# When the retention outputs of a two-layer hybrid step are issued: two lanes started earlier, gating statistics read from a copy, pooling split over two turns

## The chip, the cores and the metric

The kernel runs on one core of one Trainium2 chip. The metric is the device time of one launch in microseconds (us). The time before is 1567.13 us, the median of three runs (1566.71 to 1568.31).

Engines are named as in the profile: PE is TensorE, PEld its weight loads, DVE VectorE, ACT ScalarE, POOL GpSimd, SP the queue that issues most DMAs. Each engine carries out its own instructions strictly in the order in which they were written; between engines there are only semaphores.

## The reference

Two layers of a hybrid network work on 640 tokens of width 1024: one chunk of 128 context tokens and four chunks of 128 latent tokens, called chunk 0 to chunk 4. Everything is float32. Each layer projects its input once, and the columns feed four mixers:

- A: windowed attention.
- B: spatial gating. Of v, 256 wide, every token is normalised (mean and variance over the 256 values), a 128 x 128 matrix mixes the tokens of a chunk, and the result is multiplied with u.
- C: retention. For each chunk, head and direction the output is `(q k^T * decay) v + (q * q_dec) state`. It is normalised per head and multiplied with silu of a gate, and the two directions are added.
- D: pooling. Centred means over windows of 2, 4, 8 and 16 tokens minus the token itself, then a small matrix per group. Near a sequence's two ends the mean has fewer tokens, so eight columns at each edge are multiplied with a correction.

The four results go through one output projection, a residual and a layer norm, and then through a gated convolutional feed-forward block.

## The kernel before, in words

Every large product is done in three float32r passes (high part times high part, low times high, high times low). `fm_mm` (L576) makes a feature-major block of 128 output features, `tm_mm` (L840) a token-major block of one chunk by 256 features. 640 columns don't fit one PSUM bank, so each feature-major unit comes as a wide block (384 columns) and a narrow block (256 columns), 24 matmuls each. A `Stream` (L239 to L290) splits the weights ahead of use: one ACT copy `wh` and one DVE subtraction `wl` are issued whenever a unit is freed. It also puts in the matmuls of later modulations (`ada`).

The order of the work is written out by hand. Nothing is reordered after that. Between the blocks `tick()` (L1078) is called; one call is a **turn** here. Small work lies in *lanes*. A lane is a list of generators; in a turn each lane, in the order in which the lanes were added, goes on to its next `yield`. Where a generator ends, the next one of the same lane begins in the same turn.

The generators that matter:

- `ret_out(t)` (L970) is the retention output of chunk t. In four steps: **s1** four score products `A` on PE, four DVE multiplications `scd` with the decay that read PSUM, and for t > 0 two DVE multiplications `qdq` (queries times decay, SBUF to SBUF). **s2** the products `ro` on PE (first with `scd`, then with `qdq`), then on ACT the square `sq` and a copy `on`. **s3** the product `var` on PE, which needs `sq`; on ACT Ln and Exp, each with a table load, for the reciprocal root `rs`; on DVE the multiplication of `on` with `rs`. **s4** six POOL instructions that gate and add.
- `pool_mix` (L1035), once for each of two pooling units: **p1** the window sums on POOL (two for unit 0, four for unit 1); **p2** eight small edge corrections on POOL and two DVE instructions `py` (L1058, STT below) that scale the sums and subtract the token; **p3** nothing; **p4** the products `pp` on PE, held back until all five s1 have been issued (`m.scored`, L1062).
- `vb_out` (L850), after each token-major block of v: DVE statistics `bn` from PSUM, an ACT copy `vn` of the same bank, and the normalisation of the chunk before (`vb_norm`, L864). The framework lets two engines' instructions on one PSUM bank go only in the order written, so the copy waits for the statistics.

The blocks after the retention state are: four gate units (two directions, two halves), two pooling units, five v blocks, and the wide blocks of u. The blocks of this stretch are called Ga and Gb (wide and narrow block of the last gate unit), P0a, P0b, P1a, P1b (the two pooling units), V0 to V4 (the v blocks). A turn has the name of the block it follows. Lane X has chunks 0, 2, 4, lane Y chunks 1, 3. Before, the turns hold:

| turn | lane X | lane Y | pooling 0 | pooling 1 |
|---|---|---|---|---|
| P0a | 0 s1 | | | |
| P0b | 0 s2 | 1 s1 | p1 | |
| P1a | 0 s3 | 1 s2 | p2 | |
| P1b | 0 s4, 2 s1 | 1 s3 | p3 | p1 |
| V0 | 2 s2 | 1 s4, 3 s1 | waits | p2 |
| V1 | 2 s3 | 3 s2 | waits | p3 |
| V2 | 2 s4, 4 s1 | 3 s3 | p4 | p4 |
| V3 | 4 s2 | 3 s4 | | |
| V4 | 4 s3 (s4 follows at L1228) | | | |

Layer 1 has in front of these lanes another one, `affine_late` (two DVE instructions a turn, until turn P1b).

Of the kernel before, what the change touches and what calls it, by code (L numbers as in the profile page):

```python
# [8 lines left out]
F32 = mybir.dt.float32  # L9
# [5 lines left out]
P = 128  # L15
# [6 lines left out]
HD = 64  # L22
# [5 lines left out]
POOL_WINDOWS = (2, 4, 8, 16)  # L28
# [61 lines left out]
def kernel(  # L90
# [6 lines left out]
    V, S, G, T = nc.vector, nc.scalar, nc.gpsimd, nc.tensor  # L97
# [14 lines left out]
    def nm(p):  # L112
        cnt[0] += 1
        return f"{p}{cnt[0]}"
# [9 lines left out]
    def small(n, name="s"):  # L124
        return sm.tile([P, n], F32, tag=f"s{n}", name=nm(name))
# [722 lines left out]
        return ps  # L848

    def vb_out(m, t, ps):  # L850
        bn = sm.tile([P, 6], F32, tag="bn1", name=nm("bn1"))
        V.bn_stats(out=bn, in_=ps)
        mv = small(2, "mv")
        V.bn_aggr(out=mv, in_=bn)
        if t % 2 == 0:
            m.vnu = unit([P, 2, 256], name="vn")
        v = m.vnu[:, t % 2, :]
        S.activation(out=v, in_=ps, func=AF.Copy)
        vb_norm(m)
        m.owed = (t, v, mv, rstd_of(mv[:, 1:2]))  # L860
        if t == NT - 1:
            vb_norm(m)
# [172 lines left out]
    def pool_mix(m, prm, pt, x):  # L1035
        n = 664
        lo, hi = 1, n
        s = unit([P, n], name="p2")
        G.tensor_tensor(out=s[:, 1:n], in0=x[:, 0:n - 1], in1=x[:, 1:n], op=ALU.add)
        levels = {2: s}  # L1040
        for w, sh in ((4, 1), (8, 2), (16, 4)):
            if w > POOL_WINDOWS[2 * pt + 1]:
                break
            lo, hi = lo + sh, hi - sh
            s2 = unit([P, n], name=f"p{w}")
            prev = levels[w // 2]
            G.tensor_tensor(out=s2[:, lo:hi], in0=prev[:, lo - sh:hi - sh], in1=prev[:, lo + sh:hi + sh], op=ALU.add)
            levels[w] = s2
        y = unit([P, n], name="py")
        yield  # L1050
        for a in range(2):
            w = POOL_WINDOWS[2 * pt + a]
            r = slice(a * HD, (a + 1) * HD)
            s = levels[w]
            for e, (c, stp) in enumerate(((8, 136), (128, 520))):
                for cc in (c, c + stp):
                    G.tensor_tensor(out=s[r, cc:cc + 8], in0=s[r, cc:cc + 8], in1=m.pf[r, pt, e, :], op=ALU.mult)
            V.scalar_tensor_tensor(out=y[r, 8:656], in0=s[r, 8:656], scalar=1.0 / w, in1=x[r, 8:656],  # L1058
                                   op0=ALU.mult, op1=ALU.subtract)
        yield  # L1060
        yield
        while m.scored < NT:  # L1062
            yield
        for c, k, yo in ((8, P, 0), (144, NLAT, P)):
            ps = bank(k, name="pp")
            for a in range(2):
                r = slice(a * HD, (a + 1) * HD)
                T.matmul(ps[r, :], m.pw[r, pt, :], y[r, c:c + k], start=True, stop=True,
                         tile_position=(a * HD, a * HD))
            S.activation(out=y8[:, 6 + pt, yo:yo + k], in_=ps, func=AF.Copy, scale=prm[:, 32 + pt:33 + pt])  # L1070
# [4 lines left out]
    def lane(*gens):  # L1075
        lanes.append(list(gens))
# [18 lines left out]
    def mixers(l, m, prm, mid=None, then=None, aff=None):  # L1095
        dma = side if l else load
        attn_setup(m, l, side)
        pool_setup(m, l, dma)
        ret_loads(m, l, dma)
        m.vn, m.vc, m.g, m.scored, m.owed = {}, {}, {}, 0, None  # L1100
        raws = [y8[:, 0, :], y8[:, 1, :], unit([P, W], name="k"), unit([P, W], name="v")]
        us = [ws.take(), ws.take()]

        def start_a(*ii, mid=None, then=None):
            if ii[0] == len(us):
                us.append(ws.take())
            pss = fm_mms([us[i] for i in ii], *GA, lag=1, mid=mid)
            if then:
                then()
            for i, ps in zip(ii, pss):  # L1110
                S.activation(out=raws[i][:, 0:SPLIT_COL], in_=ps, func=AF.Copy)

        def start_b(i):
            ps = fm_mm(us[i], *GB)
            S.activation(out=raws[i][:, SPLIT_COL:W], in_=ps, func=AF.Copy)
            if i < 3:
                rope(m, raws[i])
            ws.free()
            tick()

        start_a(0, 1, mid=mid, then=then)
        yield
        start_a(2)
        yield
        ws.advance()
        if l == 0:
            attn_setup2(m)
            start_b(0)
            start_b(1)
            start_a(3)  # L1130
        else:
            start_a(3)
            yield
            ws.advance()
            attn_setup2(m)
            start_b(0)
            start_b(1)
        lane(ret_setup(m, l))
        start_b(2)
        start_b(3)  # L1140
        m.k = raws[2]
        m.kh, m.kl = [[unit([P, W], name=n).bitcast(F32R) for _ in range(2)] for n in ("kh", "kl")]
        key_split(m.k, m.kh, m.kl)

        def keep(o):
            u = ws.take()
            ps = fm_mm(u, *GA)
            S.activation(out=o[:, 0:SPLIT_COL], in_=ps, func=AF.Copy)
            tick()
            ps = fm_mm(u, *GB)  # L1150
            V.tensor_copy(out=o[:, SPLIT_COL:W], in_=ps)
            ws.free()
            tick()
            return o

        def vals(fn):
            u2 = [ws.take(), ws.take()]
            for t in range(NT):
                fn(m, t, tm_mm(t, u2))
                if t == NT - 1:  # L1160
                    ws.free(2)
                tick()

        m.kc = [y8[:, 6, :], y8[:, 7, :]]
        u = ws.take()
        ps = fm_mm(u, *GA)
        S.activation(out=m.kc[0][:, 0:SPLIT_COL], in_=ps, func=AF.Copy)
        tick()
        ps = fm_mm(u, *GB)
        V.tensor_copy(out=m.kc[0][:, SPLIT_COL:W], in_=ps)  # L1170
        at = attn_block(m, 1, True)
        next(at)
        attn_values(m, raws[3], l)
        lane(at, attn_block(m, 3), attn_block(m, 0))
        ws.free()
        tick()
        u = ws.take()
        ps = fm_mm(u, *GA)
        S.activation(out=m.kc[1][:, 0:SPLIT_COL], in_=ps, func=AF.Copy)
        tick()  # L1180
        at = attn_block(m, 2, True)
        next(at)
        lane(at, attn_block(m, 4))
        ps = fm_mm(u, *GB)
        V.tensor_copy(out=m.kc[1][:, SPLIT_COL:W], in_=ps)
        ws.free()
        tick()
        vals(vc_out)
        lane(ret_states(m, l))
        m.qc = []  # L1190
        for i in range(2):
            m.qc.append(keep(unit([P, W], name="qc")))
            if i == 0 and aff:
                lane(affine_late(*aff))
        lane(sgu_setup(m, l))
        for d in range(2):
            for p in range(2):
                g = y8[:, 4 + p, :] if d == 0 else unit([P, W], name="g")
                u = ws.take()
                for lo, hi in (GA, GB):  # L1200
                    ps = fm_mm(u, lo, hi)
                    S.activation(out=g[:, lo:hi], in_=ps, func=AF.Silu)
                    if hi == W:
                        G.tensor_scalar(out=g, in0=g, scalar1=prm[:, 34 + d * 2 + p:35 + d * 2 + p], scalar2=None,
                                        op0=ALU.mult)
                        ws.free()
                    tick()
                m.g[p, d] = g
        lane(ret_out(m, 0), ret_out(m, 2), ret_out(m, 4))
        xs_ = []  # L1210
        for i in range(2):
            u = ws.take()
            pa = fm_mm(u, *GA)
            tick()
            pb = fm_mm(u, *GB)
            x = pool_in(pa, pb)
            ws.free()
            if i == 0:
                lane(ret_out(m, 1), ret_out(m, 3))
            lane(pool_mix(m, prm, i, x))  # L1220
            tick()
        vals(vb_out)
        uu = [ws.take(), ws.take()]
        pa = [fm_mm(u, *GA) for u in uu]
        sgu(m)
        for p in range(2):
            sgu_gate(p, pa[p], *GA)
        while lanes:  # L1228
            tick()
        y_split(0)  # L1230
        y_split(1)
        for p in range(2):
            ps = fm_mm(uu[p], *GB)
            sgu_gate(p, ps, *GB)
            ws.free()
            tick()
# [153 lines left out]
    for l in range(DEPTH):  # L1390
        m = Mix()
# [214 lines left out]
```

## Time and profile before

| | us | share of the span |
|---|---|---|
| median of three runs | 1567.13 | |
| the profiled execution, its time | 1567.93 | |
| its span | 1566.2 | |
| PE busy | 1530.4 | 98% |
| DVE busy | 955.8 | 61% |
| ACT busy | 620.3 | 40% |
| POOL busy | 391.7 | 25% |

The span is the time from the first to the last instruction; 1.7 us of the execution lie around it. In the rows further down, a timeline row has its start, its duration, engine, line, operation, output and inputs, how many instructions it merges, and in brackets the idle time of the engine just before it and what ended that. A row of the stretches has, after the two ends, the length, then busy time (and instructions) of PE, PEld, DVE, ACT and POOL, the granted clock of PE (1.00 is 2.4 GHz, 0.50 is 1.2 GHz), and two columns on DMA.

### The profile page before, as it was taken

Reading aid. Unit: us, or ns where it says so; the run is one execution under the profiler, and the core shown is the slowest. Engines: PE = TensorE matmul, PEld = TensorE weight load, DVE = VectorE, ACT = ScalarE, POOL = GpSimd, SP = SyncE. Lnnn points to the kernel's source line nnn. Section 1 sums busy time; section 2 is a strip of 40 time slices with the busy share of each in tenths; the row PEclk is TensorE's granted clock in tenths of the full one; section 3 lists DMA queues with packets and bytes.
Section 4 is the critical chain, followed back from the end, with each engine's and each line's share of the span. In section 5 each row is a group of like instructions: output and inputs, shape, how many; then the busy total and the mean of one; then the engine's idle time right before and its main releaser. Section 6 shows DMA issues by size and latency. Waiting matters only on the chain.

```text
span 1566.2 us, 24540 instructions
## 1 busy us (share of the span) xinstructions
PE 1530.4 (98%) x9708; PEld 1354.3 (86%) x9708; DVE 955.8 (61%) x1886; ACT 620.3 (40%) x1004; POOL 391.7 (25%) x472
## 2 busy tenths in 40 slices
PE   6999999999999999999999999999999999999997
PEld 1988868899999999978789888688999999998885
DVE  2775255686555655754567666567866666674456
ACT  2644454244333333443346444524433333343331
POOL 2402266154101101110014035633531101020104
PEclk9999999999999999999999999999999999999999
DMA  9544415145443434243206446161332221224411
GB/s 336 159 164 142 148 58 201 55 137 168 141 148 122 150 120 161 83 144 107 89 28 197 153 141 205 55 201 55 122 107 82 81 81 55 81 89 134 133 36 67
DMA packets 120031, 193.23 MB, mean 123 GB/s; under 512 B 11812, under 2 KB 78174, under 8 KB 119917
## 3 DMA queue, kind: packets, MB, share of 16 engines
q1 hardware_dynamic: 110957, 165.65, 31.6%
q0 software_dynamic: 8960, 26.02, 5.3%
q8 instruction: 76, 1.25, 0.3%
q14 instruction: 38, 0.31, 0.1%
HBM read 177.98 MB, written 13.66 MB: 122 GB/s over the span
## 4 chain that ended last, share of the span: by engine, by line
PE 80%; DVE 3%; ACT 1%; issue 1%; POOL 1%; POOLq 0%; ACTq 0%; DVEq 0%
PE fm L571 16%; PE fm L573 15%; PE fm L572 15%; PE dn L1513 6%; PE dn L1512 6%; PE dn L1511 6%; PE wo L1420 2%; PE wo L1422 2%; PE wo L1421 2%; PE ada L233 2%; PE tm L845 1%; PE hT L540 1%; PE tm L846 1%; PE tm L847 1%; PE PT L820 0%
## 5 line engine op out<-in xcount | busy, mean ns | idle before, releaser
L571 PE MATMUL fm<-hh,wh 128*128 128x256 f32 (+1 forms) x1920 | 600.0, 313 | 1.6 <-ACT hh L1339 1.6
L573 PE MATMUL fm<-hl,wh 128*128 128x256 f32 (+1 forms) x1920 | 593.7, 309 | 2.7 <-DVE hl L1344 1.8
L572 PE MATMUL fm<-hh,wl 128*128 128x256 f32 (+1 forms) x1920 | 593.2, 309 | 0.0
L571 PEld LDWEIGHTS fm<-hh,wh 128*128 128x128 f32 x1920 | 362.2, 189 | 30.6 <-ACT cv L1260 11.7
L246 DVE TENSOR_TENSOR wl<-st,wh 128x1024 fp32r<-128x1024 f32 x186 | 278.4, 1504 | 165.3 <-ACT wh L245 164.5
L573 PEld LDWEIGHTS fm<-hl,wh 128*128 128x128 f32 x1920 | 361.7, 188 | 4.6 <-DVE hl L1344 2.8
L572 PEld LDWEIGHTS fm<-hh,wl 128*128 128x128 f32 x1920 | 361.9, 189 | 0.1
L245 ACT ACTIVATE wh<-st 128x1024 fp32r<-128x1024 f32 x188 | 196.1, 1053 | 205.8 <-PE dn L1512 141.9
L1250 DVE SCALAR_TENSOR_TENSOR cv<-fm,cwT,cv 128x127 f32<-128x127 f32 x352 | 122.0, 409 | 109.8 <-ACT cv L1247 109.8
L1512 PE MATMUL dn<-wl,hh 128*128 128x512 f32 x440 | 174.4, 396 | 0.0
L1513 PE MATMUL dn<-wh,hl 128*128 128x512 f32 x440 | 173.9, 395 | 0.3 <-DVE hl L1447 0.2
L1511 PE MATMUL dn<-wh,hh 128*128 128x512 f32 x440 | 173.7, 395 | 0.0
L1247 ACT ACTIVATE cv<-fm,cwT 128x384 f32<-128x384 f32 x88 | 58.8, 672 | 204.1 <-PE fm L573 188.6
L1460 POOL TENSOR_TENSOR act<-cv,cv 128x640 f32<-128x640 f32 x28 | 45.6, 1629 | 301.2 <-DVE cv L1265 258.7
L1260 ACT ACTIVATE cv<-fm,cwT 128x255 f32<-128x255 f32 x88 | 49.5, 563 | 176.1 <-PE fm L573 176.1
L1513 PEld LDWEIGHTS dn<-wh,hl 128*128 128x128 f32 x440 | 82.6, 188 | 21.0 <-DVE hl L1447 1.1
L1511 PEld LDWEIGHTS dn<-wh,hh 128*128 128x128 f32 x440 | 82.6, 188 | 20.1
L1512 PEld LDWEIGHTS dn<-wl,hh 128*128 128x128 f32 x440 | 82.6, 188 | 19.5
L1261 DVE SCALAR_TENSOR_TENSOR cv<-fm,cwT,bnd 128x1 f32<-128x1 f32 x88 | 19.2, 218 | 89.1 <-ACT cv L1260 88.9
L1460 POOL TENSOR_TENSOR y<-cv,cv 128x640 f32<-128x640 f32 x16 | 26.8, 1676 | 182.8 <-DVE cv L1265 182.8
L1420 PE MATMUL wo<-wh,hh 128*128 128x512 f32 x160 | 64.6, 404 | 0.0
L1422 PE MATMUL wo<-wh,hl 128*128 128x512 f32 x160 | 63.1, 395 | 0.0
(297 smaller groups left out, 2007.8 us busy)
## 6 DMA issues: line engine op xcount, KB each, us to landing
st<-in_ffn_up_dram SPq DMA_DIRECT2D x44, 1024.0 KB
wa<-in_w_ada_dram SPq DMA_DIRECT2D x80, 512.0 KB
st<-in_ffn_down_dram SPq DMA_DIRECT2D x88, 256.0 KB
st<-in_w_in_dram SPq DMA_DIRECT2D x20, 1024.0 KB
st<-in_w_ada_dram SPq DMA_DIRECT2D x16, 512.0 KB
xr<-xd POOLq DMA_DIRECT2D x30, 256.0 KB, 6.3
st<-in_w_out_dram SPq DMA_DIRECT2D x24, 256.0 KB
xd<-xr SPq DMA_DIRECT2D x20, 256.0 KB
```

The lines of the kernel that those rows point to most:

```text
L245: S.activation(out=oh, in_=view, func=AF.Copy)
L246: eng.tensor_tensor(out=ol, in0=view, in1=of, op=ALU.subtract)
L571: T.matmul(ps, wh[:, k, :], hh[:, k, lo:hi], start=(k == 0), stop=False)
L572: T.matmul(ps, wl[:, k, :], hh[:, k, lo:hi], start=False, stop=False)
L573: T.matmul(ps, wh[:, k, :], hl[:, k, lo:hi], start=False, stop=(k == KD - 1))
L1250: V.scalar_tensor_tensor(out=o[:, a + d:b - 1 + d], in0=ps[:, a + 1 - d:b - d], scalar=cwT[:, tap, f:f + 1], in1=o[:, a + d:b - 1 + d], op ...
L1420: T.matmul(ps, hh[:, k, c0:c0 + P], wh[:, k % 2, :], start=(k == 0), stop=False)
L1422: T.matmul(ps, hl[:, k, c0:c0 + P], wh[:, k % 2, :], start=False, stop=(k == KD - 1))
L1460: G.tensor_tensor(out=dst, in0=a, in1=g, op=ALU.mult)
L1511: T.matmul(ps, hh[:, s_, c0:c0 + P], wh[:, k % 2, :], start=(k == 0), stop=False)
L1512: T.matmul(ps, hh[:, s_, c0:c0 + P], wl[:, k % 2, :], start=False, stop=False)
L1513: T.matmul(ps, hl[:, s_, c0:c0 + P], wh[:, k % 2, :], start=False, stop=(k == KF - 1))
```

## The change

It has three parts. Lane X begins ahead of the last gate unit, and lane Y directly behind it instead of after the first pooling unit. In `vb_out` the ACT copy and the normalisation of the chunk before come first, and the statistics read the copy in SBUF. In `pool_mix` the two STT move out of p2 into p3, one turn behind the edge corrections. No product, DMA or shape is added or removed.

```diff
@@ vb_out
-        bn = sm.tile([P, 6], F32, tag="bn1", name=nm("bn1"))
-        V.bn_stats(out=bn, in_=ps)
-        mv = small(2, "mv")
-        V.bn_aggr(out=mv, in_=bn)
         if t % 2 == 0:
             m.vnu = unit([P, 2, 256], name="vn")
         v = m.vnu[:, t % 2, :]
         S.activation(out=v, in_=ps, func=AF.Copy)
         vb_norm(m)
+        bn = sm.tile([P, 6], F32, tag="bn1", name=nm("bn1"))
+        V.bn_stats(out=bn, in_=v)
+        mv = small(2, "mv")
+        V.bn_aggr(out=mv, in_=bn)
@@ pool_mix
                     G.tensor_tensor(out=s[r, cc:cc + 8], in0=s[r, cc:cc + 8], in1=m.pf[r, pt, e, :], op=ALU.mult)
-            V.scalar_tensor_tensor(out=y[r, 8:656], in0=s[r, 8:656], scalar=1.0 / w, in1=x[r, 8:656],
+        yield
+        for a in range(2):
+            w = POOL_WINDOWS[2 * pt + a]
+            r = slice(a * HD, (a + 1) * HD)
+            V.scalar_tensor_tensor(out=y[r, 8:656], in0=levels[w][r, 8:656], scalar=1.0 / w, in1=x[r, 8:656],
                                    op0=ALU.mult, op1=ALU.subtract)
-        yield
         yield
         while m.scored < NT:
@@ mixers
         for d in range(2):
             for p in range(2):
+                if d + p == 2:
+                    lane(ret_out(m, 0), ret_out(m, 2), ret_out(m, 4))
                 g = y8[:, 4 + p, :] if d == 0 else unit([P, W], name="g")
...
-        lane(ret_out(m, 0), ret_out(m, 2), ret_out(m, 4))
-        xs_ = []
+        lane(ret_out(m, 1), ret_out(m, 3))
         for i in range(2):
...
             ws.free()
-            if i == 0:
-                lane(ret_out(m, 1), ret_out(m, 3))
             lane(pool_mix(m, prm, i, x))
             tick()
```

## Rows read from the trace of the kernel before

**Rows 1.** Waits of PE: engine, line, releaser; us in total, times, longest us.
```profile
PE var L1014 <- ACT sq L1009: 5.5, 2, 3.3
PE ro L1006 <- DVE qdq L990: 1.6, 2, 1.0
```

**Rows 2.** Timelines of PE, layer 0 and layer 1, at the two longer waits.
```profile
226.06 2.08 PE L1014 MATMUL var<-sq,bd 128*128 128x512 f32 x2 [3.29 <-ACT sq L1009]
...
996.78 1.98 PE L1014 MATMUL var<-sq,bd 128*128 128x512 f32 x2 [2.23 <-ACT sq L1009]
```

**Rows 3.** Chain that ended last, layer 0: start us, us, what.
```profile
219.86 0.83 DVE py L1058
220.73 0.44 DVE bn L852
221.19 0.39 ACT vn L858
```

**Rows 4.** Stretches behind the waits, layer 0 and layer 1, and one with short waits.
```profile
226.06:232.50 6.44, 6.44 (x19) 2.16 (x19) 3.93 (x12) 5.79 (x9) 5.08 (x9) 0.51 0.00 0
...
996.78:1001.78 5.00, 5.00 (x18) 1.71 (x19) 3.25 (x12) 4.75 (x7) 3.72 (x7) 0.66 0.01 3
...
980.00:985.00 5.00, 3.37 (x39) 2.38 (x38) 4.89 (x9) 0.52 (x2) 3.60 (x5) 1.00 0.38 133
```

**Rows 5.** Timeline of PE, layer 0, narrow block P1b to the products behind V0.
```profile
201.52 0.38 PE L571 MATMUL fm<-hh,wh 128*128 128x256 f32 x1
...
204.56 0.71 PE L976 MATMUL A<-qc,y 64*128 64x128 f32 x8
205.20 1.13 PE L1014 MATMUL var<-sq,bd 128*128 128x512 f32 x2
206.26 1.07 PE L233 MATMUL ada<-wa,scT 128*32 128x512 f32 x8
207.25 0.39 PE L845 MATMUL tm<-wh,hh 128*128 128x256 f32 x1
...
210.32 1.09 PE L1000 MATMUL ro<-scd,vc 128*64 128x128 f32 x16
```

**Rows 6.** Timeline of ACT, layer 0, the same stretch.
```profile
202.12 0.58 ACT L1009 ACTIVATE sq<-ro 128x512 f32<-128x512 f32 x1
...
203.07 0.28 ACT L1030 ACTIVATE px<-fm 128x128 f32<-128x128 f32 x1
203.23 0.40 ACT L1031 ACTIVATE px<-fm 128x256 f32<-128x256 f32 x1
204.66 0.38 ACT L1032 ACTIVATE px<-fm 128x256 f32<-128x256 f32 x1 [1.04 <-PE fm L573]
204.94 1.05 ACT L245 ACTIVATE wh<-st 128x1024 fp32r<-128x1024 f32 x1
206.01 1.28 ACT L1016 ACT_TABLE_LOAD   x1
...
209.31 0.63 ACT L1017 ACTIVATE rs<-rs 128x512 f32<-128x512 f32 x1
```

**Rows 7.** Timeline of DVE, layer 0 (first five) and layer 1.
```profile
202.24 0.69 DVE L1018 TENSOR_TENSOR on<-on,rs 128x512 f32<-128x512 f32 x1 [5.29 <-ACT rs L1017]
202.85 1.84 DVE L1058 SCALAR_TENSOR_TENSOR py<-p,px 64x648 f32<-64x648 f32 x2
...
207.38 1.40 DVE L982 TENSOR_TENSOR scd<-A,Dt 128x256 f32<-128x256 f32 x4
208.70 2.03 DVE L990 TENSOR_TENSOR qdq<-qc,qd 128x256 f32<-128x256 f32 x2
210.66 1.76 DVE L1018 TENSOR_TENSOR on<-on,rs 128x512 f32<-128x512 f32 x1
...
968.77 0.76 DVE L990 TENSOR_TENSOR qdq<-qc,qd 128x256 f32<-128x256 f32 x2
...
980.27 3.23 DVE L990 TENSOR_TENSOR qdq<-qc,qd 128x256 f32<-128x256 f32 x2
```

## The prediction

> **What bounds the kernel now.** I read the busy table first: PE is busy for 98% of the span, so only what stops PE, or makes it work slower, can move the time. Next come PE's waits [rows 1]. Apart from the kernel's start, where PE waits for its first DMAs, two kinds are left, both in the stretch of the change: `var` waits for the square from ACT twice, 5.5 us in all, and `ro` waits for `qdq` twice, 1.6 us. The timeline puts the first kind in turn V2 of either layer, 3.29 and 2.23 us [rows 2]; the second kind is in layer 1 only, at V0. The chain of waits [rows 3] says why `var` is late: STT waits on DVE for POOL's edge corrections, `bn` stands behind STT, the ACT copy behind `bn`, and Ln, Exp and the square behind the copy. Last I read the clock: after these waits PE is granted 0.51 for 6.44 us and 0.66 for 5.00 us, while the stretch with the 1.6 us of short waits keeps 1.00 [rows 4]. The slow clock costs 6.44 x 0.49 = 3.16 and 5.00 x 0.34 = 1.70 us.
>
> All that the change can remove is therefore 3.29 + 3.16 in layer 0 and 2.23 + 1.70 + 1.6 in layer 1: **12.0 us**.
>
> **What the change removes.** The three parts cut the old chain in three places, and I believe each cut. The ACT copy has no DVE instruction ahead of it any more; STT comes a turn after its corrections; and chunk 3's s3 comes a turn earlier. So the 12.0 us go. `bn` from SBUF instead of PSUM and its place behind the normalisation are DVE work that nothing on PE waits for; I put them at 0 (the cover is the v block of the next chunk, 3.07 us [rows 5]). No DMA moves past another; POOL's loads after the stretch have six gating instructions less in front of them, but only DVE's residual waits for these, also 0.
>
> **What it brings.** The new turns have to be written out, because a lane's position against the other is what changes:
>
> Ga: 0 s1. Gb: 0 s2. P0a: 0 s3, 1 s1. P0b: 0 s4 + 2 s1, 1 s2, p1 of unit 0. P1a: 2 s2, 1 s3, p2. P1b: 2 s3, 1 s4 + 3 s1, p3 (STT), p1 of unit 1. V0: 2 s4 + 4 s1, 3 s2, p4 of unit 0, p2 of unit 1. V1: 4 s2, 3 s3, p3 of unit 1. V2: 4 s3, 3 s4, p4 of unit 1.
>
> X starts two turns earlier, Y only one. Before, a chunk's s1 shared a turn with a later step of Y and came first; now Y's s1 shares its turn with X's s3 and comes second. DVE is in order, so `scd` of chunk 3 stands behind the multiplication of chunk 2, which waits for Ln and Exp on ACT. This is the new wait, and behind it in DVE's queue are `qdq` of chunk 3 and STT of unit 0, for which PE waits too.
>
> *Wait 1, turn V0: `ro` of chunk 3.* Zero is the end of `ro` of chunk 2 in P1a.
> PE until it wants chunk 3's `scd` [rows 5]: var 1.06, narrow block 3.04, var 1.06, A 0.64, ada 0.99, V0 3.07, A 0.64: 10.50 us.
> ACT [rows 6]: handover 0.05; sq and on 0.95 (202.12 to 203.07); Ln and Exp with their table loads 3.93 (206.01 to 209.94) for chunk 1; the three copies of the pooling input 0.16 + 0.40 + 0.28; wh 1.07; another 3.93 for chunk 2: 10.77. Then DVE [rows 7]: the multiplication, 0.69 alone and 1.76 beside POOL's window sums; two of four `scd`, 0.70; two handovers of 0.05: 12.26 to 13.33. PE waits 1.8 to 2.8 us; I take 2.8, since POOL then works on unit 1's four sums, as it did beside the row of 1.76. Its second group of products wants the other two `scd`: 0.70 less the 0.27 of the first group, 0.43. The second half wants `qdq`, a pair of which took 0.76, 2.03 and 3.23. From the last `scd`, PE alone needs 0.82 + 1.09 = 1.91; with 2.03 it ends at 2.03 + 0.05 + 0.55 = 2.63, so 0.7 more (0 and 1.9 at the ends). I take 2.03, the row of layer 0 beside the same sums. Wait 1: 2.8 + 0.43 + 0.7 = **3.9** (2.2 to 5.1).
>
> *Wait 2, same turn: `pp` of unit 0.* STT is behind `qdq` on DVE: 2.03 + 1.84 + 0.05 = 3.92 against PE at 2.63: **1.3** (0.7 with the short `qdq`).
>
> *Wait 3, turn V2: `pp` of unit 1.* Its STT is in V1 behind the multiplication of chunk 3. Zero is the end of `ro` of chunk 4. PE: var 1.06, V2 3.07, var 1.06: 5.19. The others: 0.05 + 0.95 + 3.93 on ACT, then 0.05 + 0.69 + 1.84 + 0.05 on DVE: 7.56. Wait 3: **2.4** (2.2 with two STT of 0.83 [rows 3], 3.4 with a multiplication of 1.76). I take 0.69, because POOL has no sums left then.
>
> *Turn P0b, `ro` of chunk 1.* From the end of var PE needs 0.64 + 3.04 + 0.64 + 0.27 = 4.59 until the second group; the others 0.05 + 2.65 (the table is loaded ahead) + 0.05 + 0.69 + 1.40 + 0.05 = 4.89: 0.3 in layer 1 (up to 1.4). In layer 0 a modulation's products lie between; 0.
>
> *Clock.* Both old waits over 2 us brought a slow stretch, 1.70 and 3.16 us; the short ones none. Wait 3 gets 1.70, the price of the 2.23. After wait 1 PE waits for DVE again anyway, so half of that, 0.85. Together 2.55 a layer; the ends are 0 and 2 x 3.16 = 6.3.
>
> **Sum.** Per layer 3.9 + 1.3 + 2.4 + 2.55 = 10.15; twice, and 0.3: 20.6. Less the 12.0: **+8.6 us**. The profiled execution took 1567.93 us; 0.8 us over the median of 1567.13. On the median the forecast is 1575.7, say **1576 us**. All low ends: 2 x 5.1 - 12.0 = -1.8. All high ends: 2 x (5.1 + 1.3 + 3.4 + 6.3) + 1.4 - 12.0 = +21.6.
>
> A rule to weigh here. The pairs of `qdq` differ by what POOL does: 0.76 beside edge corrections, 3.23 beside window sums, while `scd` with an input in PSUM keeps its 1.40 [rows 7]. The Trainium skill (SBUF — State Buffer, section "Who interferes with whom") says that a DVE instruction with two SBUF inputs and a POOL instruction that reads SBUF exclude each other, and that whichever started first holds the port to its end. If DVE lost each such race in V0, wait 1 would be at its upper end, 1.2 more a layer, and the time 1578; the rows here show pairs that lost and pairs that did not.
>
> **Rivals.**
> *The lanes keep out of each other's way, faster.* The old 12.0 go and nothing comes: 1555. This is decided on ACT: with 1.8 us less between the two ends (10.77 down to 9.0) wait 1 would be gone, and with 2.4 us less wait 3. The only pieces of that size are the table loads, 2 x 1.28 in each s3. Were they not needed in the new order, both waits would vanish. Against it: Ln and Exp still alternate as before.
> *Low ends, no change.* POOL's sums end before the multiplication of chunk 2, and no wait is long enough for the clock: -1.8, 1565.3. For it: POOL's gating of chunk 1 also begins earlier. Against: the sums can't start before that gating.
> *The waits as summed, but the clock stays high:* 2 x 7.6 + 0.3 - 12.0 = +3.5: 1570.6. For it: the waits come in pieces with work between. Against: 2.23 us was enough.
> *High ends:* 1589, if both waits lower the clock for as long as in layer 0.
>
> **How the numbers follow.** A measurement of this kernel can tell about 0.2%, 3 us, from no change. My forecast with its neighbours (+3 to +16) has 0.60, the clock that stays high 0.13, the low ends 0.10, the faster rival 0.11, the high ends 0.06. The second lies on the border, so slower gets 0.60 + 0.06 + half of it: 0.72; within 0.2% 0.17; faster 0.11. The range reaches from the low ends to short of the high ones, 1566 to 1584; the likeliest case alone has 1570 to 1583.
>
> **What would show it.** Right: `var` no longer waits for `sq` in V2; the ACT copies have no wait for `bn`, STT none for POOL; and in both layers `ro` waits for `scd` in V0 by 2 to 3 us, `pp` for `py` in V0 and V2 by about 1 and 2.4, with the granted clock below 1 after V0 or V2. Ln and Exp of chunks 1 and 2 stand on ACT in turns P1a and P1b with only copies between. Wrong: no wait of `ro` for `scd`, or ACT through with chunk 2 before V0 ends.

## The result, and the profile after

The changed kernel is slower: 1575.39 us, the median of five runs (1574.38 to 1579.40), against 1567.80 for the kernel before (five runs, 1566.71 to 1568.61). The ratio is 1.0052, with a 95% interval of 1.0038 to 1.0067, so +6.0 to +10.5 us; the medians differ by 7.6. The forecast was 1576.

The span grew by 6.4 us, from 1566.2 to 1572.6, and PE's busy time by 1.4, from 1530.4 to 1531.8: most of the longer span is idle time of PE. First the busy table of the changed kernel:

```profile
PE 1531.8 (97%) x9708; PEld 1357.2 (86%) x9708; DVE 958.9 (61%) x1886; ACT 620.9 (39%) x1004; POOL 388.0 (25%) x472
```

PE's waits in the stretch of the change (they answer to [rows 1]; the wait for `sq` is gone, that for `qdq` stayed, and the waits of `pp` and of the first products of `ro` are new):

```profile
PE pp L1071 <- DVE py L1062: 5.5, 7, 2.0
PE ro L1000 <- DVE scd L982: 2.7, 1, 2.7
PE ro L1006 <- DVE qdq L990: 2.2, 3, 1.0
...
PE ro L1000 <- ACT vn L854: 1.8, 1, 1.8
```

The timeline of PE shows where each is. The rows up to 221.51 are turn V0 of layer 0, the two at 236 and 237 are V2; from 989.07 on it is layer 1, V0 and V2 again:

```profile
215.86 1.77 PE L1000 MATMUL ro<-scd,vc 128*64 128x128 f32 x16 [1.82 <-ACT vn L854]
...
218.22 0.65 PE L1006 MATMUL ro<-qdq,S 64*64 64x128 f32 x8 [0.59 <-DVE qdq L990]
219.91 0.65 PE L1006 MATMUL ro<-qdq,S 64*64 64x128 f32 x8 [1.04 <-DVE qdq L990]
220.74 0.40 PE L1071 MATMUL pp<-py,pw 64*64 64x128 f32 x2 [0.18 <-DVE py L1062]
221.51 2.36 PE L1071 MATMUL pp<-py,pw 64*64 64x128 f32 x6 [0.37 <-DVE py L1062]
...
236.25 0.40 PE L1071 MATMUL pp<-py,pw 64*64 64x128 f32 x2 [1.95 <-DVE py L1062]
237.02 1.29 PE L1071 MATMUL pp<-py,pw 64*64 64x128 f32 x6 [0.37 <-DVE py L1062]
...
989.07 2.45 PE L1000 MATMUL ro<-scd,vc 128*64 128x128 f32 x16 [2.72 <-DVE scd L982]
...
993.13 0.65 PE L1006 MATMUL ro<-qdq,S 64*64 64x128 f32 x8 [0.56 <-DVE qdq L990]
994.73 1.29 PE L1071 MATMUL pp<-py,pw 64*64 64x128 f32 x6 [0.42 <-DVE py L1062]
...
1007.73 0.43 PE L1071 MATMUL pp<-py,pw 64*64 64x128 f32 x2 [1.81 <-DVE py L1062]
1008.59 1.29 PE L1071 MATMUL pp<-py,pw 64*64 64x128 f32 x6 [0.43 <-DVE py L1062]
```

DVE's timeline of the same V0 and V2 (layer 0), and of V0 in layer 1, says why; it answers to [rows 7]. The multiplication of `on` waits for Ln and Exp, and `scd`, `qdq` and `py`, whose inputs were ready, stand behind it:

```profile
214.61 0.77 DVE L1018 TENSOR_TENSOR on<-on,rs 128x512 f32<-128x512 f32 x1 [2.72 <-ACT rs L1017]
215.30 1.41 DVE L982 TENSOR_TENSOR scd<-A,Dt 128x256 f32<-128x256 f32 x4
216.63 3.23 DVE L990 TENSOR_TENSOR qdq<-qc,qd 128x256 f32<-128x256 f32 x2
219.78 1.68 DVE L1062 SCALAR_TENSOR_TENSOR py<-p,px 64x648 f32<-64x648 f32 x2
...
234.68 0.69 DVE L1018 TENSOR_TENSOR on<-on,rs 128x512 f32<-128x512 f32 x1 [5.93 <-ACT rs L1017]
235.29 1.68 DVE L1062 SCALAR_TENSOR_TENSOR py<-p,px 64x648 f32<-64x648 f32 x2
...
986.92 1.67 DVE L1018 TENSOR_TENSOR on<-on,rs 128x512 f32<-128x512 f32 x1 [0.97 <-ACT rs L1017]
988.52 1.41 DVE L982 TENSOR_TENSOR scd<-A,Dt 128x256 f32<-128x256 f32 x4
989.84 3.23 DVE L990 TENSOR_TENSOR qdq<-qc,qd 128x256 f32<-128x256 f32 x2
```

On ACT Ln and Exp of chunk 1 and of chunk 2 follow each other with only copies between them and a table load ahead of each function, as in [rows 6]; of ACT's timeline, the Ln loads and the Exps:

```profile
205.04 1.28 ACT L1016 ACT_TABLE_LOAD   x1
...
208.34 0.63 ACT L1017 ACTIVATE rs<-rs 128x512 f32<-128x512 f32 x1
...
209.56 1.07 ACT L245 ACTIVATE wh<-st 128x1024 fp32r<-128x1024 f32 x1
210.65 1.28 ACT L1016 ACT_TABLE_LOAD   x1
...
213.94 0.63 ACT L1017 ACTIVATE rs<-rs 128x512 f32<-128x512 f32 x1
```

Last the clock, in stretches behind V0 and V2 of layer 0, then V0 and V2 of layer 1, as in [rows 4]:

```profile
221.00:227.00 6.00, 5.63 (x30) 3.88 (x29) 4.07 (x11) 2.03 (x4) 4.37 (x13) 0.72 0.55 178
234.00:241.00 7.00, 4.67 (x32) 3.36 (x32) 4.58 (x9) 5.63 (x9) 3.35 (x6) 1.00 0.00 0
988.00:994.00 6.00, 4.23 (x33) 3.06 (x34) 5.97 (x9) 0.38 (x1) 5.02 (x5) 0.72 0.30 104
1008.00:1014.00 6.00, 5.57 (x30) 4.60 (x29) 2.85 (x7) 3.24 (x5) 4.70 (x9) 0.72 0.00 0
```

Three of the four hold a slow part, 6.00 x 0.28 = 1.7 us each.

### The profile page after: what moved, and what is told of

It is laid out like the page before. It is cut to its first block, busy times and chain, and to the rows that moved or that the text cites. A ratio compares the mean times of both kernels' runs of the same rounds, so it can differ in the third digit from the quotient of the medians.

```text
span 1572.6 us, 24553 instructions
## 1 busy us (share of the span) xinstructions
PE 1531.8 (97%) x9708; PEld 1357.2 (86%) x9708; DVE 958.9 (61%) x1886; ACT 620.9 (39%) x1004; POOL 388.0 (25%) x472
## 4 chain that ended last, share of the span: by engine, by line
PE 90%; DVE 4%; ACT 2%; DMA 2%; issue 1%; SPq 0%; POOL 0%; POOLq 0%; ACTq 0%; DVEq 0%
PE fm L571 18%; PE fm L573 17%; PE fm L572 17%; PE dn L1515 6%; PE dn L1514 6%; PE dn L1513 6%; PE ada L233 2%; PE wo L1422 2%; PE wo L1424 2%; PE wo L1423 2%; DMA st<-in_w_ada_dram 1%; PE tm L845 1%; PE tm L846 1%; PE tm L847 1%; PE PT L820 1%
```

## The experiments

Medians below are of five runs or more beside the kernel before on the same chip; ratios are against it. Its median was 1566.84 for the first four kernels, 1567.53 for the next four and 1567.46 for the last three, so a difference between two medians of different groups, or from the 1575.39 above, is good to about 1 us.

**One part alone, and two without the third.** `e1_stats_only`, `e2_pool_only` and `e3_lanes_only` are the kernel before with one part of the change; `e4_stats_pool` has the first two. The parts are the three pieces of the diff shown above.

> The kernel before with the statistics read from the copy alone. Theory (the loss comes from the lanes alone, the two other parts only cut the old chain): the square no longer stands behind the statistics, so var's two waits and their slow clock go: 3.29 + 3.16 + 2.23 + 1.70 = 10.4 us less, about 1557; the 1.6 us of ro waiting for qdq in layer 1 stay. Rival (reading the copy in SBUF puts DVE behind ACT and costs): 0 to 3 us slower than before, 1567 to 1571.

> The kernel before with the edge corrections one turn ahead of the scaling alone. Theory: the same chain is cut at another link (DVE no longer waits for POOL ahead of the statistics), so about 1557 here too, and not the sum with the other part. Rival (the scaling, one turn later, becomes what the pooling products wait for, as in the changed kernel): pp waits about 2 us a layer, 1562 to 1567.

> The kernel before with the two lanes moved alone. Theory: ro of chunk 3 waits for scd in V0 by 2 to 3 us in both layers; pp does not wait (the scaling stands a turn earlier); var no longer waits, since chunk 3's s3 comes a turn earlier: 2 x (3.9 + 0.85 to 1.7) - 12.0 + 0.3 = -2 to 0, 1565 to 1567. Rival (the loss is in the pooling or the statistics part): the lanes alone gain 5 us or more, at or below 1562.

> The changed kernel with the lanes put back where they were. Theory: the old waits of var are gone and nothing new comes: 1556 to 1558, as with either part alone, and 18 us faster than the changed kernel. Rival (the two parts cost something themselves): more than 2 us slower than the better one of them alone.

| kernel | us | ratio, interval |
|---|---|---|
| e1, statistics | 1556.65 | 0.9937 (0.9925 to 0.9950) |
| e2, STT a turn later | 1559.44 | 0.9954 (0.9941 to 0.9966) |
| e3, lanes | 1571.48 | 1.0031 (1.0019 to 1.0043) |
| e4, statistics and STT | 1558.71 | 0.9947 (0.9935 to 0.9960) |

The statistics alone win 10.2 us. `e1` has the lowest median of all kernels here, below the kernel before and the changed one, although its interval overlaps those of `e2` and `e4`. The 1.6 us of `ro` waiting for `qdq` in layer 1, which I expected to stay, are gone too. PE's only wait in its stretch is this:

```profile
PE tm L845 <- DVE scd L982: 0.9, 1, 0.9
```

The same stage (from the last gate unit to the mixing of the spatial gating) of the kernel before, layer 0, and of `e1`, both layers; columns as in [rows 4]:

```profile
178.00:251.00 73.00, 69.72 (x545) 55.24 (x543) 34.53 (x67) 37.86 (x55) 43.00 (x73) 0.95 0.21 70
```
```profile
178.00:245.00 67.00, 67.00 (x552) 54.77 (x552) 35.46 (x67) 37.91 (x55) 44.42 (x75) 1.00 0.26 82
942.00:1009.00 67.00, 66.01 (x535) 53.75 (x535) 41.74 (x74) 36.73 (x54) 48.53 (x79) 1.00 0.38 124
```

PE is busy for 67.00 of 67.00 us at full clock in layer 0: 10.2 of the 12.0 us can be had, and by one of the three edits alone. `e2` cuts the same old chain at another link, less well: it is 2.4 us above what I expected, `var` still waits 1.7 us once, and `pp` doesn't wait, so it is not the rival. The two don't add, since they remove the same wait. `e4` is 0.7 us above its range and 2.06 us above `e1`, at the edge of what its rival says (the parts cost something themselves); the intervals overlap, so this stays open. From `e4` the full change differs by the lanes alone, and it is 1575.39 - 1558.71 = 16.7 us slower.

`e3` came out about 5 us above what I expected. `var` no longer waits and `ro` waits for `scd`, as expected, but I had not seen that without the statistics' part the earlier lanes let the normalisation of `vn` on POOL be late for the products `sg` behind the stage; its waits:

```profile
PE sg L901 <- POOL vn L872: 4.9, 2, 3.2
PE ro L1000 <- DVE scd L982: 4.7, 2, 2.8
```

`e7` below is `e3` with the statistics' part added: it has no wait of `sg` and takes 6.4 us less (1571.48 - 1565.06). So the 4.9 us came with the early lanes and the copy behind the statistics together (`e9` below has 1.5 us of this wait without the second). By which chain it comes late was not traced: POOL was busy for 18.09 of the 20 us from 236 to 256, but for 17.13 in the kernel before, where `sg` doesn't wait.

**Does the order of the two lanes cause wait 1?** `e5_swap` is the changed kernel with lane Y ahead of lane X in each turn, so that chunk 3's `scd` is issued before chunk 2's multiplication. `e6_both_early` is the changed kernel with X ahead of Y as it was, and with Y begun one turn earlier.

```diff
@@ e5_swap
-        lane(ret_out(m, 1), ret_out(m, 3))
+        lanes.insert(len(lanes) - 1, [ret_out(m, 1), ret_out(m, 3)])
@@ e6_both_early, behind the tick() of the gate units
+                    if d + p == 2 and lo == 0:
+                        lane(ret_out(m, 1), ret_out(m, 3))
...
-        lane(ret_out(m, 1), ret_out(m, 3))
```

> The changed kernel with lane Y ahead of lane X within each turn: the same steps in the same turns, only their order in a turn is turned round. Theory (order on DVE and ACT): scd of chunk 3 is then ahead of the multiplication that waits for Ln and Exp, the chain of chunk 3 starts ahead of ro of chunk 4, so all three waits go: 1556 to 1559. Rival 1 (the lanes start too early, turns are overloaded whatever their order; ACT's 10.8 us against PE's 10.5 us): 1572 to 1576. Rival 2 (only the wait for scd goes, pp still waits): 1564 to 1567.

> The changed kernel with lane Y begun one more turn earlier (behind Ga), so that the lanes stand to each other as before the change. Theory (the offset of the lanes is what costs, not how early they begin): no wait of ro for scd, 1556 to 1560. Rival (starting early costs by itself): 1572 or more.

`e5` takes 1562.46 us (0.9968, 0.9956 to 0.9980), `e6` 1560.20 us (0.9952, 0.9939 to 0.9964): the same instructions in another order are 13 and 15 us faster than the change. DVE's timeline of `e5` at V0 has the two the other way round, and `ro` no longer waits for `scd`:

```profile
212.39 1.41 DVE L982 TENSOR_TENSOR scd<-A,Dt 128x256 f32<-128x256 f32 x4
213.72 3.24 DVE L990 TENSOR_TENSOR qdq<-qc,qd 128x256 f32<-128x256 f32 x2
216.88 0.68 DVE L1018 TENSOR_TENSOR on<-on,rs 128x512 f32<-128x512 f32 x1
```

Its `qdq` pair is as long as in the full change, but costs PE only 1.0 us in all. `e6` is at the upper end of what I expected, with one wait of `ro` for `scd` left (0.6 us), where I expected none; `e5` is 3.5 us above what I expected. `pp` still waits: for `py` 0.8 us in `e5` and 1.6 in `e6`, and in `e5` once 1.5 us for nothing that the profile shows. Each has one stretch at a lower clock.

**Is it the one multiplication?** `e9_mult_late` is the changed kernel with that instruction behind the `yield`, at the head of s4: it is issued a turn later, when Ln and Exp are done.

```diff
-        V.tensor_tensor(out=on, in0=on, in1=rs.rearrange(...), op=ALU.mult)
         yield
+        V.tensor_tensor(out=on, in0=on, in1=rs.rearrange(...), op=ALU.mult)
```

> The changed kernel with the DVE multiplication of a retention chunk moved from the end of s3 to the head of s4, one turn later; nothing else moves. Theory (that multiplication, waiting for Ln and Exp at the head of DVE's queue, is what holds up scd of chunk 3 and the scaling of both pooling units): all three waits go, 1556 to 1560. Rival (ACT is too full in P1a and P1b, and PE waits for ACT itself): var or the ACT copies hold PE, 1570 or more.

1562.12 us (0.9969, 0.9957 to 0.9982), with no slow stretch: 13 us for the place of one instruction per chunk. The order of the work on every other engine is as in the change. What waits remain are short pieces:

```profile
PE pp L1071 <- DVE py L1062: 2.3, 4, 0.6
...
PE sg L901 <- POOL vn L872: 1.5, 2, 0.8
...
PE ro L1006 <- DVE qdq L990: 0.6, 2, 0.4
PE ro L1000 <- DVE scd L982: 0.3, 1, 0.3
```

The waits of `ro` and `pp` fell from 12.2 us to 3.2. So waits 1 to 3 have one cause: an instruction that waits for ACT at the head of DVE's queue. The time is 2 us above the range that I expected; the pieces left come to 4.7 us, with `sg` among them, for which PE didn't wait in the change.

**What STT in the later turn adds.** `e7_lanes_stats` is the changed kernel with STT back in p2.

> The changed kernel with the scaling of the pooling back in the turn of its corrections. Theory: the wait for scd in V0 stays (2 to 3 us and the qdq behind it), the waits of pp go and with them the second slow stretch: 2 x (1.3 + 2.4 + about 1.7) = 10.8 less than the changed kernel, 1563 to 1567, as with the lanes alone. Rival (the scaling waits for POOL again and holds up DVE in V0): 1570 or more.

1565.06 us (0.9984, 0.9975 to 0.9992), within the range that I expected. Wait 1 stays and the waits of `pp` are gone:

```profile
PE ro L1000 <- DVE scd L982: 4.7, 2, 2.8
...
PE ro L1006 <- DVE qdq L990: 1.0, 2, 0.6
```

The later STT thus costs 10 us with the early lanes (1575.39 - 1565.06) and about 2 us without (1558.71 - 1556.65, where the intervals overlap): it is in a bad place behind the waiting multiplication. Of the 10 us, waits 2 and 3 are 5.5, and the waits for `qdq` are 1.2 shorter. The clock, which I had expected to give back a slow stretch, gave nothing: PE is granted 0.57 from 218 to 226 us and 0.79 from 984 to 992 in `e7`, 8 x 0.43 + 8 x 0.21 = 5.1 us, as much as in the change. The rest was not traced, so the number came out with a term that did not. Without the later STT the early lanes still cost 1565.06 - 1556.65 = 8.4 us.

**Is it a buffer?** In the changed kernel ACT's copy `vn` in V0 waits for a large SBUF buffer (0.89 us in layer 0, 4.24 us in layer 1). A rival was that the copies ahead of Ln and Exp are late for that reason. `e8_slots` adds one buffer, `NU = 26` for 25.

> The changed kernel with 26 instead of 25 of the large buffers. In the changed kernel's trace ACT's copy of V0 waits until a buffer comes free (0.89 us in layer 0, 4.24 us in layer 1). Theory: this wait is beside the waits for scd, qdq and the scaling: within 1 us of the changed kernel, 1574 to 1576. Rival (buffers cause the waits): 3 us or more faster, at or below 1572.

1578.49 us (1.0066, 1.0053 to 1.0078), above the 1574 to 1576 that I expected. The copy of layer 0 no longer waits, that of layer 1 still does (1.91 us), and the kernel is not faster. In layer 0 `ro` waits as long as before, and now the row names `scd`, so buffers are not the cause of wait 1 there (in layer 1 the change's own row names `scd`):

```profile
217.12 2.44 PE L1000 MATMUL ro<-scd,vc 128*64 128x128 f32 x16 [1.88 <-DVE scd L982]
```

`pp` waits 4.5 us and `ro` 6.3 in its profile, and PE is granted a lower clock in four stretches. That it is 3 us slower than the change is not clear of noise: the intervals of the two ratios overlap.

**The length of the multiplication and of `qdq`.** POOL's window sums of unit 1 work beside them. `e10_sums_late` moves all steps of that unit one turn on; `e11_split_late` frees the weights of unit 1 behind turn P1b instead of ahead of it, so that the ACT copy `wh` comes behind chunk 2's Ln and Exp.

```diff
@@ e10_sums_late, head of pool_mix
+        if pt == 1:
+            yield
@@ e11_split_late
-            ws.free()
+            if i == 0:
+                ws.free()
             lane(pool_mix(m, prm, i, x))
             tick()
+            if i == 1:
+                ws.free()
```

> The changed kernel with all steps of pooling unit 1 one turn later, so that POOL has no window sums beside the multiplication of chunk 2 and qdq of chunk 3. Theory (POOL's sums lengthen these two on DVE): the pair of qdq takes about 1.2 instead of 3.23 us, and the waits of ro for qdq in V0 go, 1.6 us in layer 0 and about as much in layer 1; wait 3 moves from V2 to V3 and stays: 1571 to 1574. Rival (the pair is long for another reason): qdq keeps 3 us and the time stays 1575.

> The changed kernel with the freeing of the second pooling unit's weights, and so ACT's copy wh (1.07 us) and its DVE subtraction, behind turn P1b instead of ahead of it. Theory (ACT's queue from the square of chunk 2 to Exp of chunk 2 sets wait 1): that wait shrinks by about 1.1 us in each layer: 1572.5 to 1574. Rival (wait 1 is set by POOL or by buffers): the time and the wait stay, 1575; or slower, if the weights come late.

`e10`: 1574.65 us (1.0050, 1.0037 to 1.0063), not distinct from the change, where I expected 1571 to 1574. The pair of `qdq` took 0.75 us in both layers instead of 3.23, and no wait of `ro` for it is left; but STT of unit 1 came a turn later as well, wait 3 grew to the longest of all, and PE was granted 0.72 over the 12 us around it in either layer (234 to 246 and 1008 to 1020 us), where the change has 0.72 over 6 us in layer 1 and no slow clock in layer 0:

```profile
216.75 0.75 DVE L990 TENSOR_TENSOR qdq<-qc,qd 128x256 f32<-128x256 f32 x2
```
```profile
PE pp L1073 <- DVE py L1064: 7.8, 5, 3.7
PE ro L1000 <- DVE scd L982: 4.0, 3, 1.8
```

`e11`: 1575.47 us (1.0050, 1.0037 to 1.0064), not the 1 to 3 us less that I expected, though its five runs spread over 5.5 us. The first products of `ro` wait 1.0 us less in either layer, which is the copy of 1.07 us, so wait 1 is ACT's work as the prediction counted it:

```profile
214.40 1.77 PE L1000 MATMUL ro<-scd,vc 128*64 128x128 f32 x16 [0.80 <-ACT vn L854]
...
987.15 1.77 PE L1000 MATMUL ro<-scd,vc 128*64 128x128 f32 x16 [1.77 <-DVE scd L982]
```

But the waits for `qdq` rose from 2.2 to 3.3 us, those of `pp` stayed at 5.5, and the slow stretches are still three: the gain at the first wait of a row of waits was taken back by the next.

## Why the prediction was right

**What was removed.** Right. No `var` waits for `sq`, the copy no longer waits for `bn` (in V0 it waits for a buffer instead) nor STT for POOL. `e1` and `e2` show that one link of the old chain would have been enough; the prediction counted the three cuts together and did not ask which was needed. The 12.0 us are a price worked out from rows: the most that any run here got back is the 10.2 us of `e1`.

**Wait 1.** Predicted 3.9 a layer. Layer 0: 1.82, then 0.68 within the first products (1.77 where 1.09 is the row without a wait), 0.59 and 1.04 for `qdq`: 4.1. Layer 1: 2.72, 1.36 (2.45, part of it the slow clock), 0.56: 4.6. In layer 0 the profile names the copy `vn` for the first piece. That copy waited 0.89 us for a buffer until the same multiplication had ended, and the first of the four `scd`, which began at 215.30 and took 0.41, was through 0.15 us before the products began; `e8`, where this copy doesn't wait, has 1.88 us there and names `scd`. In layer 1, too, the products began 0.14 us behind the first `scd`, so they ask for one of the four where the sum had two.

The sum came out near, its parts did not: the multiplication took 0.77 in layer 0 where I took 1.76, and the `qdq` pair 3.23 in both layers where I took 2.03; the errors cancel in layer 0, and that is luck. The multiplication's length follows from where in a window sum of POOL it began:

```profile
213.54 1.29 POOL L1039 TENSOR_TENSOR p<-px 128x663 f32<-128x663 f32 x1
...
986.75 1.29 POOL L1039 TENSOR_TENSOR p<-px 128x663 f32<-128x663 f32 x1
```

In layer 0 this sum had 0.22 us left when the multiplication began at 214.61, in layer 1 1.12 us when it began at 986.92; in both the multiplication ended 0.55 us behind the sum. The `qdq` pair began while POOL was in its further sums in either layer and took 3.23; with the sums moved away, in `e10`, it took 0.75. The Trainium skill (SBUF — State Buffer, section "Who interferes with whom") has this as a rule: a DVE instruction with two SBUF inputs contends with a POOL instruction that reads SBUF, and the one that comes second waits. These rows agree. By that rule, with every race lost, the prediction had 1578; the shorter multiplication of layer 0 and wait 2 gave the difference back.

**Wait 2.** Predicted 1.3, measured 0.18 + 0.37 = 0.55 and 0.42. This term was mis-sized, and not because of the longer `qdq`, which moves PE and STT by the same amount. The sum let `pp` wait for both STT. In the trace the first products of `pp` (0.40 us) run as soon as the first STT is through, beside the second; the two STT took 1.68 where I took 1.84 and began 0.08 us before the end of `qdq`, and `ro` behind it took 0.65 where I took 0.55.

**Wait 3.** Predicted 2.4, measured 1.95 + 0.37 = 2.3 and 1.81 + 0.43 = 2.2. Two small errors cancel: here, too, 0.40 us of `pp` run between the two STT, and PE came to `pp` 4.8 us after the end of `ro` where the sum had 5.19.

**Turn P0b in layer 1.** Predicted 0.3; the products `ro` there took 1.39 instead of 1.09. But this is not new: the same products take 1.44 in the kernel before (at 968.33).

**Clock.** Predicted 0.85 and 1.70 a layer, 5.1 in all. Measured 1.7 three times, also 5.1, but distributed otherwise: a full slow stretch came with V0 in both layers, where I took half of one, and none behind wait 3 of layer 0 (1.95 us). In layer 0 the slow stretch begins behind the last short wait of V0 (the six products `pp` at 221.51 take 2.36 where 1.29 is the row of V2), in layer 1 within the products behind the 2.72 us. The size is a mean that came out; where the low level appears was not predicted.

**Sum.** 6.95 + 7.2 + 0.3 + 5.1 - 12.0 = +7.6 against +8.6 predicted and +7.6 between the medians; the profiled spans, from which the terms are read, differ by 1572.6 - 1566.2 = 6.4. Two entries of this sum are not clean. The 1.36 of layer 1 holds some of the slow clock that the 5.1 counts again; 0.68, as in layer 0, would be 0.7 less. And the 12.0 leave out waits inside products of the kernel before: in layer 1 those of `ro` in V0 took 1.74 and in P1a 1.44 where 1.09 is the row without a wait, 1.0 us together.

```profile
979.53 1.74 PE L1000 MATMUL ro<-scd,vc 128*64 128x128 f32 x16
```

With both the sum is +5.9. The mechanism is as predicted; an agreement to 1 us is partly luck, since each term was read in one execution and several errors cancel.

**The rivals.** The faster one asked for an ACT without second table loads; they are still there, 1.28 us each. The clock that stays high was right in one of four places. The low ends and the high ends are out: the measured interval is +6.0 to +10.5.

## What to carry to other kernels

Where small work of several chunks is interleaved in one in-order queue, write out for each turn what stands *behind* an instruction that waits for another engine; here the place of one multiplication per chunk was worth 13 us, and the order of two lanes within a turn as much. Of several edits that each cut the same chain, try each alone: one of three here had nearly all the gain, another turned it into a loss. Where several waits follow each other in a row, shortening the first alone can gain nothing: in `e11` the next ones took its time.

## What was not expected of the hardware

- A pause of PE of about 2 us does not lower the clock each time: 1.95 and then 0.37 us in V2 of layer 0 left the granted clock at 1.00, 1.81 and 0.43 us at the same place in layer 1 were followed by 0.72 over 6.00 us.
- The same two `qdq` instructions took from 0.75 to 3.24 us in these kernels, by what POOL did beside them, while four `scd`, which read PSUM, took 1.40 or 1.41 in every row shown. A DVE multiplication that began inside a window sum of POOL ended 0.55 us behind it in both layers, whether 0.22 or 1.12 us of the sum were left.
